# A batched matmul whose second load moves to SyncE's queue, and whose last store is awaited by GpSimd

## The chip, the cores and the metric

The kernel runs on one core of a Trainium2 chip. The core has five engines with a queue each: TensorE (PE in the profile, with its weight loads as PEld), VectorE (DVE), ScalarE (ACT), GpSimd (POOL) and SyncE (SP). Each engine runs its own instructions in order, and they meet by semaphores. SyncE, ScalarE and GpSimd can issue transfers, which run on the same 16 DMA engines. The metric is the device time in microseconds.

## The reference

For each of 16 batches, the product of a 512 x 512 matrix a and the transpose of a 512 x 512 matrix b, in float32:

```python
def reference(a, b):          # a: [16, 512, 512], b: [16, 512, 512]
    return np.matmul(a, b.transpose(0, 2, 1)).astype(np.float32)
```

a and b are 16.8 MB each, and so is the output: 50.33 MB cross between HBM and the core's memory.

## The kernel before

The 16 batches are worked off as 8 pairs. A load fetches two batches of one operand, 2 MB: load 0 is a of pair 0, load 1 is b of pair 0, load 2 is a of pair 1, and so on to load 15. The buffer `ld` has 7 slots (NL), load n goes to slot n modulo 7. Outputs go through `ob`, also 7 slots (NO), one batch or 1 MB each, and store n writes batch n.

For each pair VectorE casts both operands from float32 to bfloat16, half of the columns of K at a time (lines 154, 157 and 160). TensorE transposes them by a product with the identity (line 230), ScalarE copies the transposed a out of PSUM (line 189) and VectorE the transposed b (line 170). Then TensorE multiplies (line 249), and ScalarE copies the product to `ob` (line 207). VectorE, ScalarE and TensorE each run a loop over the 8 pairs, written out by hand; semaphores order them, and no scheduler moves anything.

The transfers are ordered as follows.

- At the start SyncE issues load 0 and then loads 2 to 6; ScalarE issues load 1 as its first instruction. `load(n)` (line 87) picks the queue by its argument `engine`.
- Then SyncE steps through the loads: it waits until load n has landed (line 112), signals VectorE by `s_go`, and issues load n + 6 when VectorE has cast enough to free its slot (line 94, semaphore `s_cd`).
- Stores 0 to 7 are issued by GpSimd (line 103), the first of them when the second load of slot 0, load 7, has landed (line 125). Its list `STORES` mixes the stores with waits until an earlier store has landed, by which it tells ScalarE that a slot of `ob` is free (`s_of`, line 131).
- Stores 8 to 15 are issued by SyncE, behind all the loads on its queue: 8 and 9 at step 11 of its loop, 10 and 11 at step 13, 12 and 13 at step 15, and the last two after it.
- SyncE then waits until stores 9 to 14 have landed (line 121). This ends the first critical section, a stretch of code that the framework leaves as written and puts a meeting of all engines behind.

The second critical section (line 262) has one instruction, the wait for the last store, store 15. After it comes the exit: every engine drains its queue (an instruction DRAIN) and signals GpSimd, which gathers the signals and releases the engines, clears the semaphores, and does the same again. The profile puts the exit down to line 289, and so also the wait for the last store itself.

Of the kernel before, what the change touches and what calls it, by code (L numbers as in the profile page):

```python
# [10 lines left out]
def kernel(  # L11
# [6 lines left out]
    nc = tc.nc  # L18
    P = 128
    batch, M, K = a.shape  # L20
# [8 lines left out]
    NL = 7  # L29
# [7 lines left out]
    def sbuf(name, shape, dtype):  # L37
        return ctx.enter_context(nc.sbuf_tensor(name, shape, dtype))

    def sem(name):  # L40
        return tc.alloc_semaphore(name)

    with tc.tile_critical(no_gpsimd_drain=True):  # L43
        ident = sbuf("ident", [P, P], bf16)
        one = sbuf("one", [P, 1], f32)
        ld = sbuf("ld", [P, NL, 2 * J, K], f32)
# [10 lines left out]
        s_ld = [sem(f"s_ld{i}") for i in range(NL)]  # L57
# [26 lines left out]

        def load(n, engine=nc.sync):
            u, slot = n // 2, n % NL
            src = (a if n % 2 == 0 else b)[2 * u:2 * u + 2].rearrange(
                "e (p j) k -> (e p) j k", j=2 * J  # L90
            )
            if n >= NL:

                nc.sync.wait_ge(s_cd, n - NL + 2)
            engine.dma_start(ld[:, slot], src).then_inc(s_ld[slot], 16)

        def landed(n):
            return s_st[n], 16

        def store(n):  # L100
# [3 lines left out]
                out[n].rearrange("(p j) n -> p j n", j=J), ob[:, n % NO]  # L104
            ).then_inc(s_st[n], 16)

        load(0)
        load(1, nc.scalar)
        for n in range(2, NL):
            load(n)  # L110
        for n in range(2 * pairs):
            nc.sync.wait_ge(s_ld[n % NL], 16 * (n // NL + 1)).then_inc(s_go, 1)
# [32 lines left out]
        with nc.Fori(0, pairs, engines=[dve]) as u:  # L145
            for x, (h, w, s_c, s_w) in enumerate(
                ((ha, wa, s_ca, s_wa), (hb, wb, s_cb, s_wb))
            ):
                src = ld[:, bass.ds((u * 2 + x) % NL, 1)].rearrange("p o j k -> p (o j) k")
# [110 lines left out]


    with tc.tile_critical(no_gpsimd_drain=True):
        nc.sync.wait_ge(*landed(batch - 1))


# [28 lines left out]
```

## Time and profile before

| | |
|---|---|
| Median of 3 runs | 125.48 us (125.3 to 125.67) |
| Time of the profiled execution | 125.48 us |
| Its span, first to last instruction | 123.7 us |
| Mean granted TensorE clock | 0.964 |
| Busy: PE, DVE, ACT, POOL | 90.8, 68.1, 68.0, 5.2 us |
| SyncE's queue (q1) | 39.85 MB, 76.2% of the 16 DMA engines' span |
| GpSimd's queue (q0) | 8.39 MB, 16.1% |
| ScalarE's queue (q10) | 2.10 MB, 4.2% |

The span is the time between the first and the last instruction; the execution's own time is 1.8 us more. The profile names an instruction by its line in the kernel and its engine; a q behind the engine's name (POOLq) means the engine's sequencer, which handles semaphores, branches and the issuing of transfers, and is not counted as busy. The page cuts the span into 40 slices of 3.09 us and gives for each the busy share of an engine in tenths, and what the DMA engines moved. A DMA issue is the instruction that hands a transfer to a queue; its landing is the moment when its semaphore is full, 16 signals, one from each DMA engine.

### The profile page before, as it was taken

To read this page: it belongs to the slowest core of one execution; us is meant where nothing else is said; L and a number is where in the kernel's file an instruction comes from. 1 tells how busy PE (TensorE), PEld (TensorE's weight loads), DVE (VectorE), ACT (ScalarE), POOL (GpSimd) and SP (SyncE) were. 2 spreads that over 40 slices of the span, in tenths; PEclk is the share of its full clock that TensorE was granted. 3 is DMA by queue.
4 is the path that set the end of the run, shared out by engine and by line. 5 is a ranking of instruction groups with operands and counts; after the bars stand their busy time and mean duration, and the time that the engine had idled before them with its cause. 6 is when DMAs were issued, how large, how long until landed. Compare 5 with 4: busy or idle time off the path is not lost. (4 is left out here: it accounts for less than half of the span.)

```text
span 123.7 us, 2364 instructions
## 1 busy us (share of the span) xinstructions
PE 90.8 (73%) x768; PEld 55.9 (45%) x768; DVE 68.1 (55%) x96; ACT 68.0 (55%) x130; POOL 5.2 (4%) x14
## 2 busy tenths in 40 slices
PE   0000189999999899989998999999899919995000
PEld 0000177447644754674476347645754528441000
DVE  0000698983895689289918974865957078400000
ACT  4000065478855956795589369765946069655000
POOL 2000000000000250001010110000000000000000
PEclk9999999999999999999999999999999986999955
DMA  4999999999999999999999999999999999999990
GB/s 148 413 435 429 429 429 424 429 424 435 435 424 424 429 392 363 445 416 424 453 405 437 443 408 443 424 424 458 397 445 427 408 429 427 429 427 429 424 387 8
DMA packets 4608, 50.33 MB, mean 407 GB/s; under 512 B 512, under 2 KB 512, under 8 KB 512
## 3 DMA queue, kind: packets, MB, share of 16 engines
q1 hardware_dynamic: 3312, 39.85, 76.2%
q0 software_dynamic: 1152, 8.39, 16.1%
q10 hardware_dynamic: 144, 2.10, 4.2%
HBM read 33.55 MB, written 16.78 MB: 407 GB/s over the span
## 5 line engine op out<-in xcount | busy, mean ns | idle before, releaser
L249 PE MATMUL ps<-tb,ta 128*128 128x512 bf16 x256 | 57.8, 379 | 0.5
L207 ACT COPY ob<-ps 128x512 f32 x64 | 34.4, 589 | 29.2 <-PE ps L249 21.3
L189 ACT COPY ta<-tp 128x512 bf16<-128x512 bf16 x64 | 32.9, 610 | 15.0 <-PE tp L230 15.0
L249 PEld LDWEIGHTS ps<-tb,ta 128*128 128x128 bf16 x256 | 24.1, 98 | 30.6 <-issue 4.0
L230 PE MATMUL tp<-ident,ha 128*128 128x128 bf16 x256 | 19.3, 228 | 18.1 <-PEq L135 18.1
L230 PEld LDWEIGHTS tp<-ident,ha 128*128 128x128 bf16 x256 | 16.3, 102 | 21.9 <-issue 20.1
L170 DVE COPY tb<-tp 128x1024 bf16<-128x1024 bf16 x32 | 21.2, 684 | 4.2 <-DVEq L135 4.2
L230 PE MATMUL tp<-ident,hb 128*128 128x128 bf16 x256 | 18.5, 230 | 3.4 <-PEq L135 3.4
L230 PEld LDWEIGHTS tp<-ident,hb 128*128 128x128 bf16 x256 | 16.3, 103 | 4.0 <-issue 4.0
L154 DVE CAST ha<-ld 128x1024 bf16 x8 | 5.5, 687 | 14.3 <-DVEq L135 14.3
L165 DVE COPY ha<-wa 128x2048 bf16<-128x2048 bf16 x8 | 5.5, 691 | 12.7 <-DVEq L135 12.7
L160 DVE CAST wa<-ld 128x2048 bf16 x8 | 9.8, 1220 | 0.0
L160 DVE CAST wb<-ld 128x2048 bf16 x8 | 9.7, 1217 | 0.0
L154 DVE CAST hb<-ld 128x1024 bf16 x8 | 5.5, 692 | 7.3 <-DVEq L135 7.3
L103 POOL DMA_DIRECT2D out_dram<-ob x8 | 4.5, 570 | 65.5 <-DMA ld<-in_b_dram 40.9
L169 DVE COPY hb<-wb 128x2048 bf16<-128x2048 bf16 x8 | 5.5, 685 | 0.1
L157 DVE CAST ha<-ld 128x1024 bf16 x8 | 5.5, 686 | 0.0
L157 DVE CAST hb<-ld 128x1024 bf16 x8 | 5.5, 686 | 0.0
L180 ACT ACT_TABLE_LOAD x1 | 1.3, 1283 | 1.5 <-SPq L43 1.5
L79 POOL TENSOR_SCALAR_AFFINE_SELECT ident<-ident 128x128 bf16<-128x128 bf16 x1 | 0.3, 283 | 0.2 <-POOL ident L77 0.2
L77 POOL MEMSET ident<- 128x128 bf16 x1 | 0.2, 204 | 0.5 <-SPq L43 0.5
L180 ACT COPY one<-const-float32-1.0 128x1 f32<-128x1 f32 x1 | 0.2, 192 | 0.0
(4 smaller groups left out, 0.4 us busy)
## 6 DMA issues: line engine op xcount, KB each, us to landing
ld<-in_a_dram SPq DMA_DIRECT2D x8, 2048.0 KB, 26.5
ld<-in_b_dram SPq DMA_DIRECT2D x7, 2048.0 KB, 29.6
out_dram<-ob POOLq DMA_DIRECT2D x8, 1024.0 KB, 28.9
out_dram<-ob SPq DMA_DIRECT2D x8, 1024.0 KB, 19.7
ld<-in_b_dram ACTq DMA_DIRECT2D x1, 2048.0 KB, 12.0
```

Source lines behind the costliest of these rows:

```text
L103: engine.dma_start(out[n].rearrange("(p j) n -> p j n", j=J), ob[:, n % NO]).then_inc(s_st[n], 16)
L154: nc.vector.tensor_copy(out=h[:, :J, :], in_=src[:, :J, :HK]).then_inc(s_cd, 1)
L157: nc.vector.tensor_copy(out=h[:, J:, :], in_=src[:, J:, :HK]).then_inc(s_c, 1)
L160: nc.vector.tensor_copy(out=w[:], in_=src[:, :, HK:]).then_inc(s_w, 1)
L165: nc.vector.tensor_copy(out=ha[:], in_=wa[:]).then_inc(s_ca, 1)
L169: nc.vector.tensor_copy(out=hb[:], in_=wb[:]).then_inc(s_cb, 1)
L170: nc.vector.tensor_copy(out=tb[:, ko, :], in_=tp[:, 2 + ko % 2].rearrange("k j p -> k (j p)"),).then_inc(s_eb, 1)
L180: nc.scalar.copy(out=one[:], in_=nc.const_aps.tensor(1.0, (P, 1), f32))
L189: c = nc.scalar.copy(out=ta[:, ko, e * J * P:(e + 1) * J * P].rearrange("k (j p h) -> k j p h", j=J, h=2), in_=tp[:, ko % 2, :, e * HP:(e ...
L207: c = nc.scalar.copy(out=dst[:, j, :].rearrange("m (p j) -> m p j", j=2 * J), in_=ps[:, j, :].rearrange("m (j p) -> m p j", j=2 * J),)
L230: t = nc.tensor.transpose(tp[:, 2 * x + g, j, :], h[:, j, g * P:(g + 1) * P], ident[:])
L249: t = nc.tensor.matmul(ps[:, j, :], ta[:, ko, (e * J + j) * P:(e * J + j + 1) * P], tb[:, ko, :].rearrange("k (j p) -> k j p", j=2 * J)[:, ...
```

## The change

Load 1, the first load of b, is issued by SyncE behind load 0, in place of ScalarE; `load` loses its argument. In the second critical section GpSimd waits for store 15, in place of SyncE. In the list of instructions ScalarE has one DMA issue less and SyncE one more, at its place in the order of the loads. SyncE's semaphore, drain and no-ops of the second section go, and GpSimd gets a semaphore and two no-ops (no drain, by the section's option `no_gpsimd_drain`) ahead of its exit drain. All other lines are as before, two line numbers lower.

```diff
-        def load(n, engine=nc.sync):
+        def load(n):
...
-            engine.dma_start(ld[:, slot], src).then_inc(s_ld[slot], 16)
+            nc.sync.dma_start(ld[:, slot], src).then_inc(s_ld[slot], 16)
...
-        load(0)
-        load(1, nc.scalar)
-        for n in range(2, NL):
+        for n in range(NL):
             load(n)
...
     with tc.tile_critical(no_gpsimd_drain=True):
-        nc.sync.wait_ge(*landed(batch - 1))
+        nc.gpsimd.wait_ge(*landed(batch - 1))
```

## The prediction

> **What bounds the kernel now.** I read the page's slices first, to see whether an engine or the transfers fill the span, then the stretches around the two places of the change, then the waits of SyncE's queue, and last the small instructions of the exit.
>
> ```profile
> span 123.7 us, 2364 instructions
> DMA  4999999999999999999999999999999999999990
> GB/s 148 413 435 429 429 429 424 429 424 435 435 424 424 429 392 363 445 416 424 453 405 437 443 408 443 424 424 458 397 445 427 408 429 427 429 427 429 424 387 8
> HBM read 33.55 MB, written 16.78 MB: 407 GB/s over the span
> ```
>
> The DMA row is 9 from the second slice to the last but one, at about 427 GB/s. 50.33 MB at that rate are 117.9 us of a 123.7 us span. No compute engine is above 73%. So the time is: when the first packet starts, plus 50.33 MB at the rate, plus what follows the last landing.
>
> ```profile
> 2.00:4.00 2.00, 0.00 (x0) 0.00 (x0) 0.00 (x0) 0.95 (x2) 0.00 (x0) 1.00 0.96 344
> 6.00:42.00 36.00, 25.52 (x224) 16.58 (x224) 22.42 (x32) 17.80 (x35) 0.00 (x0) 1.00 1.01 430
> 44.00:47.00 3.00, 2.94 (x22) 1.42 (x20) 2.72 (x5) 1.71 (x5) 0.88 (x2) 1.00 1.04 363
> 114.00:120.00 6.00, 0.00 (x0) 0.00 (x0) 0.00 (x0) 0.00 (x0) 0.00 (x0) 0.84 1.02 430
> 122.00:123.70 1.70, 0.00 (x0) 0.00 (x0) 0.00 (x0) 0.00 (x0) 0.00 (x0) 0.50 0.00 0
> ```
>
> These are stretches: from, to, length, busy time of PE, PEld, DVE, ACT and POOL, granted clock, DMA share, GB/s. From 114 on nothing computes while 430 GB/s still flow: the last store was issued at 113.7 and landed at 122.26, so compute has slack at the end. The rate falls below 430 at the start and at 44 to 47, where GpSimd has just issued its first four stores. The last 1.4 us carry no data.
>
> ```profile
> SPq L112 <- DMA ld<-in_a_dram: 19.8, 6, 9.2
> SPq L121 <- DMA out_dram<-ob: 5.7, 3, 2.4
> SPq L289 <- DMA out_dram<-ob: 1.7, 1, 1.7
> ...
> L95 SPq DMA_DIRECT2D ld<-in_a_dram x8: 327/355/531, 0.9 to 57.7; - x8
> L95 ACTq DMA_DIRECT2D ld<-in_b_dram x1: 386/386/386, 0.9 to 0.9; - x1
> 13.50 0.69 DVE L154 CAST ha<-ld 128x1024 bf16 x1 [13.50 <-DVEq L135]
> ```
>
> SyncE ends by waiting for stores; the 1.7 us wait put down to L289 is the wait for the last store, which the change moves. The first two loads are issued together at 0.9, and VectorE first works at 13.50.
>
> ```profile
> L289 POOLq DRAIN  x3: 34/129/714, 120.1 to 123.4; - x3
> L289 SPq DRAIN  x3: 7/7/7, 122.7 to 123.0; - x3
> L289 ACTq DRAIN  x2: 8/8/8, 120.1 to 123.0; - x2
> L289 POOLq EVENT_SEMAPHORE_RANGE_CLEAR  x1: 287/287/287, 123.1 to 123.1; - x1
> ...
> L278 POOLq DRAIN  x1: 186/186/186, 0.3 to 0.3; - x1
> ```
>
> The columns are count, then shortest/median/longest in ns, then first and last start. The row to see is GpSimd's drain: 714 ns for the one at 120.1, where every other engine's takes 7 to 10. It runs while SyncE still waits for the last store, so now it is free.
>
> **The change, part by part.**
>
> The sum is made against the profiled execution: span 123.7, its time 125.48, so 1.8 lie around the span; 125.48 is also the median of the three runs.
>
> *Part 1, the first load of b moves from ScalarE's queue to SyncE's.* Instructions: ScalarE loses one DMA issue (386 ns at 0.91), so its table load and the constant copy, done at 2.96, come some 0.4 earlier; ScalarE's next work is at 16.14, worth 0. SyncE gains one issue and the five loads behind it move back one issue each, 0.38 to 0.53 by its row. The last of them goes out near 3.9 instead of 3.42; its data follows 10 MB of others, 24 us of transfer. That cover makes it 0.
>
> First packet: in the trace's packet records ScalarE's queue starts at 1.933, 1.02 after its issue at 0.913. SyncE's queue, issued at 0.948, starts at 2.670, 1.72 after, but that is just when the first packets of ScalarE's queue end (2.673), so it looks like a place in line, not a slow queue. Without the other load I expect 0.948 + 1.02 = 1.97: +0.035. Ends: +0.035, and +0.74 if 2.670 is the queue's own start. I take the first.
>
> Rate at the start: 16 KB packets take 611 ns when settled. The first sixteen, one per engine, take 893 on average, 0.28 too much; over the whole start the excess is 0.34 per engine. The first 0.28 comes with any first packet; the other 0.06 falls on the first packets of the second queue and may go. I take -0.06; ends 0 and -0.34.
>
> Landings: now both loads share the engines and land at 13.06 and 12.89. In turn, the first lands near 1.97 + 0.28 + 8 x 0.611 + 0.5 for completion = 7.6, the second still near 12.9. VectorE starts near 8.1 (0.44 after landing, as 13.50 is after 13.06), casts b at about 13.2 instead of 15.84, and pair 0 leaves 2.6 earlier; pair 1 then meets load 3 (landed 22.68, its b cast now at 24.84), which leaves a lead of about 1.7. Buffers come free earlier by that, but SyncE's queue is never empty: load 15, issued at 60.05, lands at 99.49 behind the others. GpSimd's first stores still wait for load 7 (landed 42.26, by 16.8 MB of transfer), and pair 5 waits for load 11 (69.84), where the lead is gone. An earlier compute under a full DMA: 0.
>
> *Part 2, GpSimd waits for the last store in place of SyncE.* Behind the wait on GpSimd stands only the exit: its stores are issued by 71.1 and its own waits on landed stores end at 105.0. SyncE has nothing behind either. Waiting for the earlier critical section to end (SyncE's no-op at 120.33) is under the store that lands at 122.26, with 1.9 of cover. Those who wait for GpSimd are all engines, at the exit barrier, whose gather and release GpSimd performs.
>
> Now: the wait ends at 122.282; SyncE's branch, semaphore, drain, no-op take until its exit drains at 122.677 and 122.740, and GpSimd gathers at 122.772: 0.490. After: GpSimd does the branch, the semaphore and two no-ops, for which I take SyncE's 0.395 (no-op and semaphore rows are 13 and 17 ns on both), then its own exit drain, which can no longer start at 120.1 because it stands behind the wait, then 0.044 to the gather (as at the start: drain ends 0.496, semaphore 0.540). With 714 ns: 0.395 + 0.714 + 0.044 = 1.153, that is +0.66. With the shortest drain row, 34 ns: 0.473, that is -0.02. Between the ends stand 129 and 186. I take 714: it is the same instruction in the list, the first drain after GpSimd's stores, while 34 and 129 follow it and 186 precedes any DMA. Release, second barrier and range clear are as before.
>
> [...]
>
> Sum: +0.035 - 0.06 + 0.66 = +0.64, so 126.1 us.
>
> **The rivals.**
>
> *Short drain (not slower).* The 714 ns fall in the only drain that runs beside DMA traffic; those at 0.3, 122.9 and 123.4 do not, and they are short. Moved behind the last landing it may take 129 to 186: part 2 is then +0.08 to +0.14 and the time 125.5 to 125.6. It decides if the drain is below about 0.4 us (then the sum is under +0.35). Against: it is also the first drain after eight GpSimd stores, which the move doesn't alter.
>
> *Late first packet.* If SyncE's queue needs 1.72 us from issue to first packet, all 50.33 MB start 0.74 late instead of 0.035: 126.8. Against: the exact meeting of 2.670 and 2.673.
>
> *The dip at 44 to 47 changes.* Its packets take up to 820 ns on average instead of 611, about 0.6 per engine in all, between GpSimd's issue at 42.56 and the first packet of its queue at 46.93. VectorE's copies run through it, and will stand some 1.7 earlier. Gone, the time is 125.5, and with the lag of the slowest DMA engine (the last store's 16 parts land from 120.63 to 122.26) up to 0.5 less, 125.0; doubled, 126.7. I can't tell the sign from this trace.
>
> [...]
>
> **How the numbers follow.** About 0.3% (0.38 us, bounds 125.10 and 125.86) is what a measurement of this kernel tells from no change. Forecast 0.58, at 126.1, its own range 125.8 to 126.4. Short drain 0.24, at 125.55. Late packet 0.06, at 126.8. Dip smaller 0.07, at 125.0 to 125.5; larger 0.05, at 126.7. Slower: 0.53 of the forecast's 0.58, 0.06 and 0.05: 0.64. Faster: 0.04 of the smaller dip and 0.04 of the short drain with the start's full 0.34: 0.08. Same: 0.28. The range takes in the short drain and most of the dip: 125.3 to 126.6 leaves out the late packet and the ends of the dip.
>
> **What the profile of the changed kernel would show.** Right: GpSimd's exit drain starts near 122.7 and takes about 700 ns, the gather follows near 123.4; the first packet starts near 1.97; the first landing is near 7.6 and VectorE's first cast near 8.1, with the same last landing, about 122.2. The slices of the DMA row stay 9. Wrong: a drain of 200 ns or less there; a first packet at 2.6; or a last landing more than 0.3 from 122.26, which would put the cause in the transfers, not in the exit.

## The result and the profile after

The changed kernel takes 126.31 us (median of 6 runs, 126.04 to 126.72) against 125.53 us of the kernel before in the same comparison (6 runs, 125.3 to 125.8): a ratio of 1.0065, with a 95% interval of 1.0044 to 1.0087. It is slower by some 0.8 us; 126.1 was predicted. The profiled execution took 126.72 us, 0.4 above the median, and its span is 124.9 us, so its sizes are read with care and against the other profiles below.

The page of the changed kernel, the same rows as before:

```profile
span 124.9 us, 2365 instructions
DMA  5899999999999999999999999999999999999950
GB/s 110 362 430 430 420 425 435 430 441 441 425 425 420 420 430 456 388 435 438 420 454 396 456 409 435 441 409 467 391 433 441 417 425 422 425 433 428 428 223 3
```

The DMA engines are as busy as before in between. Ahead of the last two slices, which hold the end of the transfers and the exit, two places differ: the first two slices move 110 and 362 GB/s in place of 148 and 413, and the dip of slices 15 and 16 (392 and 363) is 430 and 456.

Stretches of the changed kernel (from, to, length, busy time of PE, PEld, DVE, ACT and POOL, granted clock, DMA share, GB/s):

```profile
2.00:4.00 2.00, 0.00 (x0) 0.00 (x0) 0.00 (x0) 0.54 (x2) 0.00 (x0) 1.00 1.01 238
44.00:47.00 3.00, 2.94 (x15) 1.26 (x14) 3.00 (x5) 1.50 (x3) 2.69 (x4) 1.00 0.98 415
122.00:124.90 2.90, 0.00 (x0) 0.00 (x0) 0.00 (x0) 0.00 (x0) 0.00 (x0) 0.50 0.01 3
```

And VectorE's first cast of a and of b in its timeline (start and length in us first):

```profile
9.23 0.69 DVE L152 CAST ha<-ld 128x1024 bf16 x1 [9.23 <-DVEq L133]
...
14.02 0.69 DVE L152 CAST hb<-ld 128x1024 bf16 x1 [2.36 <-DVEq L133]
```

238 GB/s where 344 were at 2 to 4, 415 where 363 were at 44 to 47, and VectorE's first cast 4.3 us earlier.

SyncE's wait at the end of the changed kernel (us in total, times, longest):

```profile
SPq L287 <- POOLq L260: 2.3, 1, 2.3
```

The exit's instructions (count, shortest/median/longest in ns, first and last start in us):

```profile
L287 POOLq EVENT_SEMAPHORE  x7: 17/17/1664, 121.0 to 124.8; - x7
L287 SPq DRAIN  x3: 7/7/7, 123.2 to 124.2; - x3
L287 POOLq DRAIN  x3: 34/130/714, 123.3 to 124.7; - x3
L287 POOLq EVENT_SEMAPHORE_RANGE_CLEAR  x1: 287/287/287, 124.3 to 124.3; - x1
```

SyncE now waits for GpSimd. GpSimd has the long wait (1664 ns), and the drain of 714 ns that began at 120.1 is the first of its three and begins at 123.3, after the wait; the range clear moves from 123.1 to 124.3. In the trace the last store lands at 122.80 and the span ends 2.12 later; before, it landed at 122.26 and the span ended 1.41 later. Of the 1.24 us between the two profiled executions, 0.71 lie behind the last landing, the exit, and 0.54 ahead of it, in the transfers.

The 0.54 are the delay of a single DMA engine. The trace has 16 signals for each of the 32 transfers, and a landing is the last of them. For the last store, fifteen are there at 121.12 before and at 121.13 after; the sixteenth comes at 122.26 and at 122.80. After the fifteenth, data packets follow one another singly, 8 KB in about 0.31 us each, until 121.78 before and 122.33 after. In the eight other kernels below that move all the data and don't run dry, this last signal is 0.91 to 1.62 us behind the fifteenth; the 1.67 of this execution is the longest.

### The profile page after: what moved, and what is told of

The parts are those of the page before. It is cut to its first block, busy times and chain, and to the rows that moved or that the text cites. A ratio compares the mean times of both kernels' runs of the same rounds, so it can differ in the third digit from the quotient of the medians.

```text
span 124.9 us, 2365 instructions
## 1 busy us (share of the span) xinstructions
PE 90.6 (72%) x768; PEld 55.6 (45%) x768; DVE 68.2 (55%) x96; ACT 68.1 (55%) x130; POOL 6.7 (5%) x14
## 5 line engine op out<-in xcount | busy, mean ns | idle before, releaser
L228 PE MATMUL tp<-ident,hb 128*128 128x128 bf16 x256 | 17.8, 225 | 7.7 <-PEq L133 7.4
L228 PEld LDWEIGHTS tp<-ident,hb 128*128 128x128 bf16 x256 | 15.7, 101 | 8.5 <-issue 8.5
L103 POOL DMA_DIRECT2D out_dram<-ob x8 | 6.0, 758 | 64.0 <-DMA ld<-in_b_dram 41.7
```

The costliest lines, as they stand in the source:

```text
L103: engine.dma_start(out[n].rearrange("(p j) n -> p j n", j=J), ob[:, n % NO]).then_inc(s_st[n], 16)
L228: t = nc.tensor.transpose(tp[:, 2 * x + g, j, :], h[:, j, g * P:(g + 1) * P], ident[:])
```

## The experiments

Three theories stood. A: GpSimd's exit drain lost its cover, and that is nearly the whole loss. B: the start on one queue costs. C: the start costs, and the earlier compute gives most of it back at 44 to 47 us. A fourth, D, comes with e5. Times are medians, ratios those to the kernel before on the same chip with a 95% interval.

**Each part alone.** e1 is the kernel before with the wait moved:

```diff
-        nc.sync.wait_ge(*landed(batch - 1))
+        nc.gpsimd.wait_ge(*landed(batch - 1))
```

> Only the wait for the last store moves to GpSimd; the first load of b stays on ScalarE's queue. Theory A (the exit drain of GpSimd, 714 ns, lost its cover): about 0.68 slower than the kernel before, 126.2 us at a before of 125.53, with a drain of about 714 ns after the last landing, the first packet near 1.93 and the loads landing as before (13.06, 12.89, 17.79). Rival B (the whole loss comes from the start on one queue): the kernel before's time, 125.5.

Measured: 126.25 us, ratio 1.0055 (1.0039 to 1.007). In its profile:

```profile
L289 POOLq DRAIN  x3: 34/130/714, 122.5 to 123.9; - x3
```

The last store lands at 122.03 and the span ends 2.12 later. The exit is 0.71 longer than before, as in the profile of both parts, and the median says +0.69. A is right for this part.

e2 is the changed kernel with the wait given back to SyncE:

```diff
-        nc.gpsimd.wait_ge(*landed(batch - 1))
+        nc.sync.wait_ge(*landed(batch - 1))
```

> Only the first load of b moves to SyncE's queue; SyncE keeps the wait for the last store. Theory A: what is left of the measured 0.78 after the drain's 0.68, that is +0.1, 125.6 us. Rival B (the start on one queue costs what the profile of the changed kernel showed, load 2 landing at 18.59 instead of 17.79): +0.5 to +0.8, 126.0 to 126.3 us. Theory A takes the slow first packets of that profile (1413 ns on average for the first sixteen, against 907) for scatter from run to run; then this profile may show either.

Measured: 125.72 us, ratio 1.0010 (0.9998 to 1.0021). The part is worth +0.1 and can't be told from nothing in this run; 0.55% and 0.10% make the 0.65% of both. B in its large form falls as to the time, but not as to the start: load 2 lands at 18.45 again, and the first sixteen packets of 16 KB take 1329 ns on average (before: 907). The slow start came back in a second kernel, and most of it does not reach the end.

**What makes the drain long.** e3 leaves GpSimd's drain at the end of the first section on:

```diff
-    with tc.tile_critical(no_gpsimd_drain=True):
+    with tc.tile_critical():
         ident = sbuf("ident", [P, P], bf16)
```

> The changed kernel, with GpSimd's drain left on at the end of the first critical section, so that GpSimd drains near 120.6, under the last store, and again at the exit. If the 714 ns belong to the first drain after GpSimd's stores, the early one takes 714 and the exit drain 34 to 190: the time comes back by 0.52 to 0.68, to 125.6 to 125.8 us. If every exit drain behind that branch takes 714 whatever came before, both take about 714 and the time stays at 126.3.

Measured: 125.67 us, ratio 1.0002 (0.9988 to 1.0015). The end of the first section (line 43) and the exit (line 287):

```profile
L43 POOLq DRAIN  x1: 714/714/714, 120.2 to 120.2; - x1
...
L287 POOLq DRAIN  x3: 34/34/130, 122.9 to 123.6; - x3
```

The early drain takes the 714 ns at 120.2, under the last store, and the exit drain behind the wait takes 34. GpSimd still waits for the last store, and the loss is gone. So it was not the wait that cost, but the drain behind it.

e4 leaves GpSimd's stores out; e11 and e12 leave out all but four, and all but one:

```diff
             engine = nc.gpsimd if n < STORES.count("S") else nc.sync
+            if engine is nc.gpsimd:      # e11: and n >= 4; e12: and n >= 1
+                engine.wait_ge(s_out, n + 1).then_inc(s_st[n], 16)
+                return
             engine.wait_ge(s_out, n + 1)
```

> The changed kernel, but GpSimd issues no store: batches 0 to 7 of the output are not written, and GpSimd signals in place of each of these stores, once its data is there. Some 8.4 MB less are moved, so the time falls to about 106 us; what counts is GpSimd's exit drain. If GpSimd's stores make it 714 ns, it takes 34 to 190 here. If it is 714 here too, the stores are not its cause. Also: the drop of the rate at 44 to 47 in the kernel before would be absent if GpSimd's stores cause it.

> The changed kernel with stores 0 to 3 issued by GpSimd as usual and stores 4 to 7 left out (batches 4 to 7 of the output are not written, GpSimd only signals). If GpSimd's exit drain costs a fixed time once it has issued a store, it takes 714 ns; if it grows with the number of stores (41 ns at none, 714 at eight, so 84 each), it takes about 380 ns.

> The same with store 0 alone issued by GpSimd and batches 1 to 7 not written. Fixed cost: 714 ns. By the number of stores: about 125 ns. The drop of the rate while GpSimd's first stores are issued (0.35 to 0.65 per engine with a burst of four, absent with none) should be a quarter or less if it goes by the number of issues.

Measured: 116.51, 116.66 and 116.07 us in one run each. The time of e4 was misjudged by 10 us: with 8.4 MB less to move, TensorE is busy for 79% of e4's span, and the page shows two slices of 0 GB/s near the end, in which the transfers wait for compute. The drains, in the order e4, e12, e11:

```profile
L290 POOLq DRAIN  x3: 34/41/117, 113.7 to 114.4; - x3
```

```profile
L290 POOLq DRAIN  x3: 34/117/135, 113.2 to 114.0; - x3
```

```profile
L290 POOLq DRAIN  x3: 34/130/387, 113.5 to 114.6; - x3
```

The first exit drain takes 41 ns with no store, 135 with one, 387 with four and 714 with eight: 82 to 94 more for each store. Each store was 1 MB, so whether it goes by their number or by their bytes can't be told. Nor does it hang on when the last of them was issued: in e9, below, GpSimd issues its last store 5 us later than the kernel before, and its drain at 120.5 takes 714 too. The stores had all been issued by 71.7 and had landed by 104.9 in the changed kernel, 18 us before the drain, so the drain does not wait for them to land.

**Whose cover it is.** e8 is the changed kernel with the wait on ScalarE:

```diff
-        nc.gpsimd.wait_ge(*landed(batch - 1))
+        nc.scalar.wait_ge(*landed(batch - 1))
```

> The changed kernel, but ScalarE waits for the last store. GpSimd then drains near 120.6 under the last store's transfer, 714 ns for nothing: the load-only kernel's 125.7, 0.6 less than the changed kernel. If it isn't the cover of GpSimd's drain that counts but that SyncE waits, it stays at 126.3.

Measured: 125.59 us, ratio 1.0004 (0.9994 to 1.0013).

```profile
L287 POOLq DRAIN  x3: 34/130/714, 120.3 to 123.5; - x3
```

GpSimd drains at 120.3 again, beside the wait. SyncE and ScalarE both do as the one that waits; VectorE and TensorE were not tried.

**The start.** The stretch from 2 to 4 us of e1 and e10 (two queues), then of e2 and e8 (one queue):

```profile
2.00:4.00 2.00, 0.00 (x0) 0.00 (x0) 0.00 (x0) 0.95 (x2) 0.00 (x0) 1.00 0.94 319
```

```profile
2.00:4.00 2.00, 0.00 (x0) 0.00 (x0) 0.00 (x0) 0.96 (x2) 0.00 (x0) 1.00 0.96 311
```

```profile
2.00:4.00 2.00, 0.00 (x0) 0.00 (x0) 0.00 (x0) 0.54 (x2) 0.00 (x0) 1.00 0.93 238
```

```profile
2.00:4.00 2.00, 0.00 (x0) 0.00 (x0) 0.00 (x0) 0.53 (x2) 0.00 (x0) 1.00 0.96 254
```

Of all profiles, the four that start on two queues (the kernel before, e1, e9, e10) have 270 to 344 GB/s there (mean 311), the ten that start on one 213 to 254 (mean 236). The difference of 75 over 2 us is 0.35 us of transfer at 430. Load 2 lands at 17.79 to 18.21 in the four and at 18.32 to 18.83 in the ten. The first sixteen packets take 907 to 1149 ns on average in the four and 1213 to 1434 in the ten. e9 and e10 were expected to start like the kernel before (900 to 1050 ns, load 2 near 17.8); with 1149 and 1090 ns, 18.17 and 18.21 they are slower than that, so the gap between the groups is smaller than the first pair of profiles shows. Two runs asked what in the one queue is slow.

e6 issues all of the first seven loads from ScalarE:

```diff
         for n in range(NL):
-            load(n)
+            load(n, nc.scalar)
```

> The load-only kernel, but all of the first seven loads are issued by ScalarE, so the start is again on one queue, the other one. If one queue is what makes the first packets slow, the first sixteen take 1300 to 1450 ns on average, load 2 lands near 18.5 and the time is 125.7. If it is SyncE's queue that is slow, they take 900 to 1050 ns and load 2 lands near 17.8, as in the kernel before; the time is then 125.2 to 125.5.

Measured: 133.49 us, ratio 1.0634 (1.0608 to 1.066). The first sixteen packets take 1318 ns on average, load 2 lands at 18.32: the start is as slow as SyncE's, so it is not SyncE's queue as such that is slow. The time was not foreseen. Loads 7 and on are on SyncE's queue and pass the waiting ones: load 7 lands at 28.32, load 4 at 39.32 and load 6 at 63.74. Compute runs dry, and at the end the transfers wait for it; from 28 to 60, and the page's rates:

```profile
28.00:60.00 32.00, 18.49 (x163) 12.72 (x161) 14.98 (x21) 13.01 (x26) 2.35 (x4) 0.79 1.01 427
```

```profile
GB/s 105 388 433 433 433 443 413 438 428 416 428 403 433 431 450 421 428 426 445 408 433 428 426 428 431 438 433 418 453 408 418 423 428 249 274 363 0 57 421 159
```

TensorE is busy for 18.49 of these 32 us, against 30.35 in the kernel before, at full transfer rate; the bill comes in the slices of 249, 274, 0 and 57 GB/s.

e7 is e2 with the later loads held back, by a wait for ScalarE's constant:

```diff
-        for n in range(NL):
+        load(0)
+        nc.sync.wait_ge(s_one, 1)
+        for n in range(1, NL):
             load(n)
```

> The load-only kernel, with load 1 and those after it issued only when ScalarE has made its constant, near 2.6, in place of 1.38. If the first packets are slow because the next loads are handed to the same queue while they run, the first sixteen take about 900 ns on average and load 2 lands near 17.9: 125.2 to 125.5. If they are slow by themselves, they stay at 1300 to 1450 ns and the time at 125.7.

Measured: 125.78 us, ratio 1.0019 (1.0006 to 1.0031); first sixteen packets 1304 ns, load 2 at 18.45. Load 1 is issued at 2.58, when most of the first sixteen packets have started (14 of them by 2.29 in the changed kernel), so what is handed to the queue behind load 0 is not the cause. What is stays open.

**Where the start's loss goes.** The drop of the rate is given below as an excess: the time that SyncE's 16 KB packets take above 611 ns each, summed and divided by 16 engines. At 43 to 49 it is 0.64 in the kernel before and 0.03 in the changed one. e5 is e2 with the first signal to VectorE held:

```diff
         for n in range(2 * pairs):
+            if n == 0:
+                nc.sync.wait_ge(s_ld[1], 16)
             nc.sync.wait_ge(s_ld[n % NL], 16 * (n // NL + 1)).then_inc(s_go, 1)
```

> The first load of b on SyncE's queue and SyncE waiting for the last store (the load-only kernel, 125.72), with VectorE's first cast held until load 1 has landed too, so that compute runs at the place of the kernel before, some 2 us later, and keeps the one-queue start. Theory C (the slow start costs about 0.5, and the earlier compute gives most of it back by a smaller drop of the rate while GpSimd issues its first stores): the drop's excess at 43 to 49 is back at 0.35 to 0.65 per engine and the time is 126.0 to 126.3. Rival D (the drop scatters from run to run, wherever compute stands): an excess anywhere from 0.04 to 0.65 and the load-only kernel's 125.7.

Measured: 125.71 us, ratio 1.0023 (1.0012 to 1.0033). The excess of the packets at 43 to 49 is 0.07 per engine, not 0.35 to 0.65. C falls in this form: with compute no longer early (VectorE's cast in pair 3 at 46.90; before, 45.49) the drop does not come back in this profile. Rival D, that the drop scatters from profile to profile, said 125.7 and any excess from 0.04 up, and fits.

e9 and e10 move GpSimd's first store in the kernel before:

```diff
-        nc.gpsimd.wait_ge(s_ld[0], 32)
+        nc.gpsimd.wait_ge(s_ld[1], 32)      # e9;  e10: s_ld[5], 16
```

> The kernel before, with GpSimd's first store waiting for load 8 (landed 47.80) in place of load 7 (42.26), so that its four issues fall some 5.5 us later. If the drop of the rate comes from these issues and depends on what VectorE does beside them, its excess changes from 0.35 to 0.65 and the time with it, down to 125.0 if it vanishes; if it only moves, the time stays at 125.5. Against a gain: the outputs leave later, and compute may wait for slots of ob.

> The kernel before, with GpSimd's first store waiting for load 5 (landed 32.47), so that each of the first four stores is issued as soon as its output is there (near 27 to 41 us by ScalarE's copies), one by one and not in a burst. If the drop needs the burst of four issues, its excess at 30 to 49 is near 0.1 and the time is 125.0 to 125.2; if each issue costs its share, the sum stays 0.35 to 0.65 and the time 125.5. Both runs also give one more start on two queues each: first sixteen packets near 900 to 1050 ns if two queues make the difference, load 2 landing near 17.8.

Measured: 125.85 us, ratio 1.0020 (1.0007 to 1.0032), and 125.83 us, ratio 1.0018 (1.0008 to 1.0027). The drop moves with the issues, to 50 to 54 in e9 and to 34 to 40 in e10, and stays at 0.3 to 0.5 per engine; at 44 to 47, where the kernel before has 363 GB/s, e9 has 426:

```profile
44.00:47.00 3.00, 2.94 (x25) 1.58 (x23) 2.50 (x6) 1.70 (x4) 0.00 (x0) 1.00 1.00 426
```

In these profiles the drop comes with GpSimd's issues. e4 alone would not show it: without any store of GpSimd its excess is 0.03 and its rate 415, which the changed kernel has too, with all its stores:

```profile
44.00:47.00 3.00, 2.94 (x15) 1.20 (x13) 3.00 (x5) 1.11 (x4) 0.00 (x0) 1.00 0.98 415
```

In e12, with one store, the excess is 0.09, in e11, with four, 0.10: in these profiles it does not go by the number of issues. That the burst makes it is not borne out either. The 125.5 that was expected if the drop only moves was missed: both versions are 0.2% slower, clear of zero. In their profiles fifteen signals of the last store are there at 121.04 and 121.13, as before, and the sixteenth comes 1.62 and 1.47 later, where it was 1.14. From 28 to 60 us, the kernel before, e9, e10 and e1 carry 421, 423, 422 and 424 GB/s; the changed kernel 431, and the other one-queue kernels with all stores (e2, e3, e5, e7, e8) 423 to 428:

```profile
28.00:60.00 32.00, 30.35 (x278) 18.82 (x276) 23.61 (x35) 23.39 (x46) 2.85 (x5) 1.00 1.01 421
```

```profile
28.00:60.00 32.00, 30.35 (x269) 18.41 (x267) 25.01 (x36) 23.09 (x46) 4.00 (x5) 1.00 1.01 431
```

The means, 422.5 and 426.8, differ by 0.32 us of transfer over 32 us. The packet records say the same in time: 12 MB have been moved at 30.81 us on average in the four kernels that start on two queues and at 31.25 in the six on one, 30 MB at 73.22 and at 73.36. So of 0.44 us that the start costs, 0.14 are left on average; by medians, e3, e8, e2, e7 and e5 stand 0.02% to 0.23% above the kernel before, the last two clear of zero. That the drop is smaller because the start was slower is not shown: each kernel has one profile, the two groups overlap, and the drop varies from 0.03 to 0.41 between kernels with the same start, as rival D has it. No run isolates why the other queue's packets are slower beside GpSimd's issues, nor why one DMA engine ends so far behind the others.

## Why the prediction was right

The direction, the size (126.1 for 126.31) and the reason given for the exit hold. The terms for the start do not, and that the sum came so near is in part luck.

*Part 2, the exit: right.* +0.66 was the term; e1 measured +0.69, the profile of the changed kernel +0.70 from the end of the wait to the gather. Its steps: the drain is 714 ns as taken, from the right one of the four rows; the way took 1.188 instead of 1.153, since the way through the semaphore and two no-ops took 0.43, not 0.395. The reason given for 714, the first drain after GpSimd's stores, is what e3 shows, but it is no fixed cost: it grows with the stores, from 41 ns at none, which no row of the kernel before could tell.

*The short drain (0.24): wrong.* The drain at 123.3 has no DMA traffic beside it (0 GB/s from 122.8 to the end of the span) and takes the same 714 ns.

*Part 1, the first packet: right.* 1.986 for 1.97; the late packet is refuted: with no other load ahead of it SyncE's queue starts 1.04 after its issue, not 1.72.

*Part 1, the rate at the start: wrong in sign.* The packet records of the kernel before give 907 ns and an excess of 0.42 per engine where the prediction read 893 and 0.34; its conclusion does not hang on that. The step took -0.06, on the ground that the second queue's first packets were an extra cost, with bounds of 0 and -0.34. The start on one queue is slower: the first sixteen packets take 1413 ns in the changed kernel, load 2 lands at 18.59 against 17.79. The bounds left out a loss. They held the 0.28 of the first sixteen for the price of any first packet, which was the author's assumption; the runs show 1213 to 1434 on one queue and 907 to 1149 on two. So the landings were late too, 8.80 and 13.69 for 7.6 and 12.9, and VectorE's first cast at 9.23 for 8.1: up to 6 us the excess is 0.99 per engine, where the step for the landing allowed 0.28.

*Earlier compute is worth nothing: right as a sum.* VectorE stands 1.4 us earlier in pair 3 (its cast at 44.12 for 45.49), and the transfers are full all the same.

*The dip changes (0.12): it did*, from 0.64 to 0.03 per engine in the profiled pair, and this rival was rightly kept, but it did not decide. Against the slower start it leaves e2's +0.1, not to be told from zero. So the sum came out because a term missed (the start) and a rival (the dip) largely cancel, which nothing in the prediction foresaw; only the exit was understood.

*The sign that was to prove it wrong*, a last landing more than 0.3 from 122.26, was met in the changed kernel's profile (122.80), in an execution 0.4 above its median. It did not point at the cause: fifteen of the sixteen signals came as before (121.13 for 121.12), the one that was late belongs to the transfers, and the kernel's loss is in the exit, by e1 and e3. The part alone (e2) has 122.62, e3 and e8 122.43 and 122.42.

## What to carry to other kernels

Look at what an engine still has to do after its last wait. Here that is GpSimd's exit drain, 714 ns where the other engines' take 7 to 10: it costs nothing while SyncE or ScalarE waits for the last store (125.72 in e2, 125.59 in e8), and it is paid in full when GpSimd does the waiting (+0.69 in e1). If GpSimd must be last, let it drain earlier, under a transfer, as in e3 (125.67). And see whether a second queue lets later loads pass earlier ones: in e6, with the first seven loads on one queue and the rest on another, load 7 landed at 28.32 and load 4 at 39.32, and 6.3% were lost. This row of loads, consumed in order, was better off on one queue; the first two on two queues, as in the kernel before, did no harm. Last, an average rate does not tell when a transfer lands: the last store landed with the slowest of its sixteen signals, 0.91 to 1.67 us behind the other fifteen in the ten kernels that move all the data and don't run dry.

## What was not expected of the hardware

- GpSimd's first drain after it has issued stores of 1 MB takes 41, 135, 387 and 714 ns after 0, 1, 4 and 8 of them, in the changed kernel 18 us after the last of the eight landed; the drains after that take 34 to 130.
- The program's first transfers run slower when they are on one queue (213 to 254 GB/s from 2 to 4 us) than on two (270 to 344), whichever of the two queues it is, by e6 (229 GB/s), and whether or not more is handed to it at once, by e7 (229 GB/s), with one profile of each kernel. The cause was not found.
- A start that costs 0.44 us leaves 0.14 on average once 30 MB are moved, in kernels whose DMA engines are busy throughout (421 to 431 GB/s from 28 to 60 us). The rate drops less beside GpSimd's first stores in the profile of the changed kernel (an excess of 0.03 us per engine, 0.64 in the kernel before); whether that is more than scatter is not shown.
- One DMA engine of sixteen brings the last store in 0.91 to 1.67 us behind the other fifteen, in the ten kernels that move all the data and don't run dry. In e4, without GpSimd's stores, the loads' last signal is never more than 0.16 behind the fifteenth; in the changed kernel, which differs from e4 in these stores alone, this grows from 0.11 or less at the first nine loads to 0.96 at the last load and 1.67 at the last store. Which engine it is, and why, no run here shows.
